# First mixer of a two-block forward pass: head projections turned from features on partitions to tokens on partitions, with the head norms along the free axis; and two steps of the opening moved

## The chip, the cores and the metric

One core of a Trainium2 chip runs the whole program in one launch. The metric is device time in microseconds (us). TensorE (PE) does the matmuls, PEld is its weight load, VectorE (DVE), ScalarE (ACT) and GpSimd (POOL) do elementwise work, and SyncE (SP) issues nearly all DMA transfers. Three runs of the kernel before took 2167.51, 2169.84 and 2172.88 us.

## The reference, cut to what matters

The program is a first transformer block, then a second block with a mixer and a mixture of experts. The change is in the first block: its mixer, and the very first norm.

```python
h = h + 0.5 * swiglu(rms_norm(h, g_ffn1[i]), ...)              # first FFN
u = rms_norm(h, g_mix[i]) @ w_in[i]                            # 512 tokens, 1024 features
q_lat, kv_lat, k_rope, qd, kd, vd = jnp.split(u, IN_OFFSETS, axis=-1)
# diff_mixer: 4 heads, two 64-wide queries and keys each, 128-wide values
q = rms_norm(qd.reshape(B, S, 4, 2, 64), g_q)
k = rms_norm(kd.reshape(B, S, 4, 2, 64), g_k)
a = softmax(q1 k1 * scale + bias) - lam * softmax(q2 k2 * scale + bias)
o = rms_norm(a @ v, g_sub) * (1 - lambda_init)
# mla_mixer: 8 heads; 64-wide nope and 32-wide rope part, each with its norm
q = (rms_norm(q_lat, g_q_lat) @ w_q_up)
kv = (rms_norm(kv_lat, g_kv_lat) @ w_kv_up)
q_nope, k_nope = rms_norm(q[..., :64], g), rms_norm(k_nope, g)
q_rot = apply_rope(rms_norm(q[..., 64:], g), cos, sin)
h = h + concat([o_mla, o_diff]) @ w_out[i]
h = h + 0.5 * swiglu(rms_norm(h, g_ffn2[i]), ...)              # second FFN
```

## The kernel before, in words

Activations are kept transposed: features on the 128 partitions, all 512 tokens along the free axis, as eight tiles h0 to h7. A matmul operand is split into a high and a low part (xs0h and xs0l, whl for weights), and one product is three matmuls, high by high, high by low and low by high (mm3, lines 400 to 402; a few low-level lines are shared by all callers, so tiles tell them apart). A weight block is a DMA of 512 KB into wraw, a copy on ACT to the high part (L377) and a subtraction for the low part, in turn on DVE (L380) and on POOL (L384).

**Opening** (setup and block1). h0 is loaded from ACT's queue, h1 to h7 from SP's. For each of the eight tiles norm_prep writes the high part on ACT (L395), the low part on DVE (L396), the square on POOL (L431) and adds it to acc on DVE (L435). The first two weight blocks (gate in psg, up in pss, 24 matmuls each) wait for these parts; eight thin matmuls with ones (L444) follow.

**First mixer** (block1, from 386 to 723 us). A projection (proj) is 24 matmuls of 512 columns, weights stationary, into one PSUM bank psg of a pool G of three; evacuate (L632) multiplies by the token's rstd, broadcast over partitions. The norm of a head is a sum over partitions, so row_rstd (L485 square on ACT, L488 thin matmuls against two indicator columns, into [token, head] form) and rsqrt give 1/rms with tokens on partitions; pairs (L462) spreads these over 128 columns, bc2 (L470) transposes them back, and diff_n (L771) and mla_n (L863, L871) multiply. Values are transposed on PE (L566), since the attention product wants tokens on partitions. The MLA heads do the same from the two latents, with a rope table on DVE (L727).

**Order.** TASKS1 lists the projections; ITEMS1 lists the eight attention items d0 to d3, m0 to m3. merge interleaves the two generators by weights in their yields, need holds an item back until its inputs are some clock units old, high_priority lifts single instructions, and the scheduler fixes one static order for each engine. The scores of an item run beside the output product of the item before; projection matmuls stand between them. In a diff item DVE does, for each of four query tiles, two bias-and-min passes (L790) and the difference (L803), ACT two exponentials (L794); the output product is L814. The pool G is used by projections, by the output products and by w_out alike.

The few lines around which the steps turn:

```python
ps = self.G()                                   # proj: one bank for a projection
self.mm3(ps, w[:, 0, c], w[:, 1, c], x[:, 0, :], x[:, 1, :], k == 0, k == kc - 1)
nc.vector.tensor_tensor(L_["y"], ps, r, op=OP.mult)          # evacuate, L632
nc.scalar.activation(sq, y, AF.Square)                       # row_rstd, L485
nc.tensor.matmul(ps[:, o : o + 2], sq[...], self.cb1[...])   # row_rstd, L488
```

Of the kernel before, what the change touches and what calls it, by code (L numbers as in the profile page):

```python
# [16 lines left out]
P = 128  # L17
T = 512
# [13 lines left out]
TASKS1 = "q1 k1 v1 v0 kv q2 k2 v2 ql0 ql1 rq q3 bq k3 ple0 rkv kr v3 wkv bkv m0 m1 ple1 m2 wo2 m3 wo3 wo0"  # L32
# [47 lines left out]
def layout(inp):  # L80
# [20 lines left out]
    cols = []  # L101
    for h in range(HD):
        cols += [oqd + h * P + ar(P), okd + h * P + ar(P), ovd + h * P + ar(P)]
    cols += [oq + ar(256), okv + ar(128), kr, krp, kr, krp]
    L["w_inA"] = _a(w_in, np.concatenate(cols))
# [9 lines left out]
    wq = _a(g["w_q_up"][0], np.concatenate(qcols))  # L115
    L["w_qup"] = np.ascontiguousarray(wq.reshape(2, 4, P, 256).transpose(0, 2, 1, 3).reshape(2, P, 1024))
# [32 lines left out]
    L["c_rt1"] = np.concatenate([c, ss, c, ss], axis=0)  # L149
# [87 lines left out]
class Prog:  # L237
# [64 lines left out]
    def setup(self):  # L302
        nc, I, base = self.nc, self.I, self.base
        self.g1 = base.tile([P, 82], F32, name="g1")
        self.h = [base.tile([P, T], F32, name=f"h{m}") for m in range(KC)]
        nc.scalar.dma_start(self.h[0], I["xT"][0])
        nc.scalar.preload_act_table_set("silu_and_others")
# [261 lines left out]
    def block1(self):  # L569
# [18 lines left out]
        rtab = self.U("rtab")  # L588
        nc.sync.dma_start(rtab, I["c_rt1"])
# [26 lines left out]
        def proj(w, evac=None, src=None, kc=KC, o=0):  # L616
            ps = self.G()
            for k in range(kc):
                c = slice(o + k * P, o + k * P + P)
                x = (xs if src is None else src)[k]  # L620
                self.mm3(ps, w[:, 0, c], w[:, 1, c], x[:, 0, :], x[:, 1, :], k == 0, k == kc - 1)
                if k % 2:
                    yield 1.3
            if evac is None and "rb" not in L_:
                L_["first"] = ps
                return
            evacuate(ps, L_["rb"] if evac is None else evac)
# [13 lines left out]

        def t_first(w):
            yield from proj(w)
            L_["r"] = self.rstd(acc2, D, "mix")

        def t_second(w):
            ps, first = self.G(), L_.pop("first")
            self.gemm(ps, w, xs, KC)
            L_["rb"] = self.bcast(L_.pop("r"), "mix")
            evacuate(first, L_["rb"])  # L650
            Y_[0] = [L_["y"]]
            evacuate(ps, L_["rb"])
            Y_[0].append(L_["y"])
            stats(("qk", 0), [(y, 0) for y in Y_[0]])
            yield

        def t_q(w, h):
            yield from proj(w)
            Y_[h] = [L_["y"]]

        def t_k(w, h):
            yield from proj(w)
            Y_[h].append(L_["y"])
            stats(("qk", h), [(y, 0) for y in Y_[h]])
            yield 1.0

        def t_v(w, h):
            yield from proj(w)
            vd[h] = self.U("vd")
            self.transposes(vd[h], L_["y"])  # L670
            mark(("v", h), 1.0)
            yield 0.4
# [32 lines left out]
        def t_b(w, k):  # L705
            L_["rb" + k] = self.bcast(L_["r" + k], k)
            yield 0.4

        def t_mla(w, p):
            if p % 2 == 0:  # L710
                L_["wq"] = w
            ql = [L_["ql", 0], L_["ql", 1]]
            ys = []
            for e in range(2):
                yield from proj(L_["wq"], L_["rbq"], ql, 2, ((2 * p + e) % 4) * 256)
                ys.append(L_["y"])
            for o in (0, 512):
                yield from proj(L_["wkv"], L_["rbkv"], [L_["kvl"]], 1, o + p * P)
                ys.append(L_["y"])
            yield 1.3  # L720
            vd["m", p] = self.U("vm")
            self.transposes(vd["m", p], ys[3])
            Y_["m", p] = ys
            stats(("m", p), [(ys[0], 1), (ys[1], 2), (ys[2], 0)])
            for e in range(2):
                rr = slice(64 * (1 - e), 64 * (1 - e) + 64)
                nc.vector.tensor_tensor(ys[e][rr], ys[e][rr], rtab[rr], op=OP.mult)  # L727
            yield 2.0
# [35 lines left out]

        def diff_n(h):
            yield from need(("qk", h))
            r = L_["qk", h]
            es = [self.pairs(r, 4, o) for o in (0, 2)]
            for y, e, g, d, n in ((Y_[h][0], es[0], gd[:, h : h + 1], q_, "dq"), (Y_[h][1], es[1], self.g1[:, GDK : GDK + 1], k_, "dk")):
                t = self.U("dn")  # L770
# [4 lines left out]
            del Y_[h]  # L775
# [31 lines left out]
        def diff_o(h):  # L807
# [3 lines left out]
            for j in range(4):  # L811
                at = self.U("at")
                self.cols(at, a, j)
                mm(po, vd[h][:, j * P : (j + 1) * P], at, start=j == 0, stop=j == 3)  # L814
                yield 1.3
# [24 lines left out]
        def mla_kr(_):  # L840
# [4 lines left out]
            nc.vector.tensor_tensor(t, t, rtab, op=OP.mult)  # L845
# [12 lines left out]
        def mla_n(p):  # L858
            yield from need(("m", p))
            ys, r = Y_.pop(("m", p)), L_["m", p]  # L860
            es = [self.pairs(r, 6, o) for o in (4, 0, 2)]
            kn = self.U("kn")
            nc.vector.scalar_tensor_tensor(kn, ys[2], self.g1[:, GMKN : GMKN + 1], self.bc2(es[0]), op0=OP.mult, op1=OP.mult)  # L863
            yield 0.4
            q_["m", p], k_["m", p] = [], []
            for e in range(2):
# [4 lines left out]
                nc.vector.scalar_tensor_tensor(t, ys[e], gs[:, e : e + 1], self.bc2(es[1 + e]), op0=OP.mult, op1=OP.mult)  # L871
# [27 lines left out]
        def mla_o(p):  # L899
            aa, r1 = M_.pop(("m", p))  # L900
            po = self.G()
            vm = vd["m", p]
            for j0 in (0, 2):
# [7 lines left out]
                for n, m in enumerate((3, 1, 2, 0)):  # L911
                    e, j, at = ats[m]
                    ins = mm(po[64 * e : 64 * e + 64], vm[:, j * P + 64 * e : j * P + 64 * e + 64], at, start=n < 2 and j0 == 0, stop=n > 1 and j0 == 2)
# [12 lines left out]
        for k in range(2):  # L926
            nc.sync.dma_start(praw[k], I["pT"][k])
        wA = I["w_inA"]
        lead = [(wA[0], t_first), (wA[1], t_second)]
        T_ = {"ql0": [(wA[12], lambda w: t_ql(w, 0))], "ql1": [(wA[13], lambda w: t_ql(w, 1))], "kv": [(wA[14], lambda w: t_kv(w, 0))],  # L930
              "kr": [(wA[15], lambda w: t_kr(w, 0))], "wkv": [(I["w_kvup"][0], lambda w: t_wkv(w, 0))]}
        for k in ("q", "kv"):
            T_["r" + k] = [(None, lambda w, k=k: t_r(w, k))]
            T_["b" + k] = [(None, lambda w, k=k: t_b(w, k))]
        for h in range(4):
            for s, f in enumerate((t_q, t_k, t_v)):
                T_["qkv"[s] + str(h)] = [(wA[3 * h + s], lambda w, f=f, h=h: f(w, h))]
            T_[f"m{h}"] = [(I["w_qup"][h // 2] if h % 2 == 0 else None, lambda w, h=h: t_mla(w, h))]
            T_[f"wo{h}"] = [(I["w_out"][h, m4], lambda w, h=h, m4=m4: t_wo(w, h, m4)) for m4 in range(2)]
        for b in range(2):  # L940
# [1241 lines left out]
```

## Time and profile before

| | us |
|---|---|
| median of three runs | 2169.84 |
| the profiled execution, its own time | 2170.61 |
| its span, first to last instruction | 2168.8 |
| PE busy in the span | 2104.8 (97%) |
| DVE, ACT, POOL busy | 957.9, 715.1, 557.1 |
| mean granted TensorE clock | 0.988 of full speed |

The profile is of one execution; busy shares say little where stages differ, so the stretches are read one by one. Durations of single matmuls overlap, since PE pipelines them; the distance between starts is what one costs. A matmul with f32 operands is recorded twice.

### The profile page before, as it was taken

How to read it: one execution, taken by the hardware profiler on the slowest of the kernel's cores; microseconds unless marked ns; L12 is line 12 of the kernel's file. 1: busy time of each engine (PE TensorE's matmuls, PEld its weight loads, DVE VectorE, ACT ScalarE, POOL GpSimd, SP SyncE). 2: the span in 40 equal slices, each digit the busy share in tenths (PEclk: the TensorE clock that was granted, in tenths of full speed). 3: DMA queues.
4: the chain of work that ended last, by engine and by line, in shares of the span. 5: the costliest groups of instructions: out<-in, count | busy, mean ns of one | idle time of the engine just before them, and what ended most of it. 6: DMA issues, size and time to landing. Idle time of an engine off the chain costs nothing.

```text
span 2168.8 us, 25911 instructions
## 1 busy us (share of the span) xinstructions
PE 2104.8 (97%) x10233; PEld 1511.1 (70%) x10233; DVE 957.9 (44%) x1695; ACT 715.1 (33%) x1193; POOL 557.1 (26%) x457
## 2 busy tenths in 40 slices
PE   7999999999899999999998999999999999999997
PEld 5888888777676788888777877667887455545544
DVE  5323334465675532323476995553253232323322
ACT  3223223445644422222344667442231111111112
POOL 4323224423421532323443445111230000000000
PEclk9999999999999999999999999999999999999999
DMA  4223333311010232333322111112626899999994
GB/s 153 93 93 97 97 97 107 120 64 51 19 49 20 89 96 88 97 97 98 110 86 75 50 37 47 30 49 69 235 67 248 351 400 414 421 411 410 413 391 163
DMA packets 67838, 330.73 MB, mean 152 GB/s; under 512 B 7792, under 2 KB 8960, under 8 KB 43648
## 3 DMA queue, kind: packets, MB, share of 16 engines
q1 hardware_dynamic: 66992, 327.71, 40.9%
q8 instruction: 82, 1.34, 0.3%
q10 hardware_dynamic: 720, 1.31, 0.2%
q14 instruction: 44, 0.36, 0.1%
HBM read 326.90 MB, written 2.10 MB: 152 GB/s over the span
## 4 chain that ended last, share of the span: by engine, by line


## 5 line engine op out<-in xcount | busy, mean ns | idle before, releaser
L384 POOL TENSOR_TENSOR whl<-wraw,whl 128x512 fp32r<-128x512 f32 x228 | 306.4, 1364 | 598.0 <-ACT whl L377 366.7
L377 ACT ACTIVATE whl<-wraw 128x1024 fp32r<-128x1024 f32 (+1 forms) x227 | 237.1, 1045 | 638.5 <-PE psg L402 264.6
L380 DVE TENSOR_TENSOR whl<-wraw,whl 128x1024 fp32r<-128x1024 f32 (+1 forms) x113 | 157.0, 1389 | 60.1 <-ACT whl L377 59.9
L2045 POOL TENSOR_TENSOR fr<-fv,mhalf 128x1 f32<-128x1 f32 x4 | 2.2, 544 | 513.9 <-DVE fv L2044 512.2
L1745 PE MATMUL pss<-mw,xe 128*64 128x512 f32 x512 | 115.3, 592 | 0.0
L1745 PE MATMUL pss<-mw,hT 128*64 128x512 f32 x480 | 109.7, 611 | 0.5 <-ACT hT L1923 0.5
L526 POOL TENSOR_TENSOR t<-t,t 128x512 f32<-128x512 f32 x44 | 57.2, 1300 | 202.0 <-DVE t L525 194.4
L1745 PE MATMUL psg<-mw,xe 128*64 128x512 f32 x480 | 108.1, 592 | 0.0
L525 DVE TENSOR_TENSOR t<-pss,rb_f 128x512 f32<-128x512 f32 x44 | 30.4, 690 | 162.8 <-PE pss L402 162.8
L558 DVE SCALAR_TENSOR_TENSOR h<-pst,h 128x512 f32<-128x512 f32 x48 | 33.2, 691 | 140.3 <-PE pst L402 140.3
L2018 DVE TENSOR_TENSOR h<-h,psg 128x512 f32<-128x512 f32 x120 | 81.1, 685 | 23.0 <-PE psg L1745 23.0
L1905 DVE SCALAR_TENSOR_TENSOR mt<-pss,sc,mt 128x512 f32<-128x512 f32 x16 | 12.0, 750 | 179.1 <-PE pss L1745 178.6
L1745 PEld LDWEIGHTS pss<-mw,xe 128*64 128x64 f32 x512 | 36.7, 137 | 73.1 <-issue 73.1
L1745 PEld LDWEIGHTS psg<-mw,xe 128*64 128x64 f32 x480 | 34.4, 137 | 68.2 <-issue 64.6
L1745 PEld LDWEIGHTS pss<-mw,hT 128*64 128x64 f32 x480 | 33.9, 140 | 65.1 <-issue 60.9
L396 DVE SCALAR_TENSOR_TENSOR yel<-pss,sc,yeh 128x512 fp32r<-128x512 f32 x32 | 24.0, 751 | 121.5 <-ACT yeh L395 121.5
L1745 PE MATMUL pst<-disp,uhh 128*128 128x256 f32 x256 | 66.7, 287 | 1.2 <-DVE disp L1823 1.2
L523 DVE TENSOR_TENSOR t<-psg,rb_f 128x512 f32<-128x512 f32 x44 | 30.4, 690 | 81.6 <-PE psg L402 76.0
L1745 PE MATMUL pst<-disp,uhl 128*128 128x256 f32 x256 | 65.2, 281 | 0.0
L1904 ACT ACTIVATE mt<-psg,sc 128x512 f32<-128x512 f32 x16 | 11.0, 687 | 157.1 <-PE psg L1745 134.2
L435 POOL TENSOR_TENSOR acc<-acc,sq 128x512 f32<-128x512 f32 x33 | 49.9, 1512 | 39.6 <-ACT sq L433 35.8
L395 ACT ACTIVATE yeh<-pss,sc 128x512 fp32r<-128x512 f32 x32 | 22.0, 688 | 115.1 <-PE pss L1745 105.0
(889 smaller groups left out, 5625.5 us busy)
## 6 DMA issues: line engine op xcount, KB each, us to landing
mw<-in_w SPq DMA_DIRECT2D x188, 1024.0 KB, 9.2
wraw<-in_w_gu SPq DMA_DIRECT2D x87, 512.0 KB, 3.5
wraw<-in_w_d SPq DMA_DIRECT2D x48, 512.0 KB, 3.5
wraw<-in_w2A SPq DMA_DIRECT2D x38, 512.0 KB, 3.5
wraw<-in_w_inA SPq DMA_DIRECT2D x16, 512.0 KB, 3.5
wraw<-in_w_out SPq DMA_DIRECT2D x8, 512.0 KB, 3.5
wraw<-in_w_pg SPq DMA_DIRECT2D x8, 512.0 KB, 3.6
wraw<-in_w_up SPq DMA_DIRECT2D x8, 512.0 KB, 3.4
```

The source lines that it names most:

```text
L377: nc.scalar.activation(hl[:, 0, :n], raw[:, :n], AF.Copy)
L380: nc.vector.tensor_sub(hl[:, 1, :n], raw[:, :n], hl[:, 0, :n].bitcast(F32))
L384: nc.gpsimd.tensor_sub(hl[:, 1, c], raw[:, c], hl[:, 0, c].bitcast(F32))
L395: nc.scalar.activation(hi, src, AF.Identity, scale=scale)
L396: nc.vector.scalar_tensor_tensor(low, src, scale, hi.bitcast(F32), op0=OP.mult, op1=OP.subtract)
L435: (eng or nc.gpsimd).tensor_add(acc, acc, t)
L523: nc.vector.tensor_tensor(t1, pg, rb, op=OP.mult)
L525: nc.vector.tensor_tensor(t2, pu, rb, op=OP.mult)
L526: nc.gpsimd.tensor_tensor(t2, t1, t2, op=OP.mult)
L558: nc.vector.scalar_tensor_tensor(self.h[m], py, 0.5, self.h[m], op0=OP.mult, op1=OP.add)
L1745: return self.next_to(nc.tensor.matmul(*args, **kw))
L2018: self.nc.vector.tensor_tensor(self.h[m], self.h[m], ps, op=OP.add)
```

## The change

All of the edits are in the first block.

- **Projections of the diff heads.** Query and key of one head form a block of 256 columns, and the values of two heads another: six blocks (w_inB), each of two weight loads, the first for input tiles 0 to 3 and the second for 4 to 7. t_block makes the activations stationary (128 tokens) and streams 256 weight columns: 96 matmuls of 256 columns into two banks of G, for four token tiles. The latents, the shared rope key and their loads (w_inA) stay as they were.
- **Norms.** squares takes the square on ACT straight from the bank and sums groups of 64 on DVE (TENSOR_REDUCE); qk multiplies by the square of the token's rstd, takes rsqrt, and scaled writes both banks times 1/rms. turned then transposes the normalised tiles, and split applies the gain on the way out of PSUM.
- **Values.** values evacuates with a per-partition scale on ACT; no transposition follows.
- **MLA.** t_up does the same from the latents, for queries of four heads (mq0, mq1), all keys (mk) and all values (mv), one bank for each token tile; the rope table is applied with the gain in mla_n.
- **Opening.** h0 comes from SP's queue, after the first half of the first weight block, and the squares are on ACT.
- **Order.** TASKS1 has a new list; the broadcasts of the latents' rstd (bq, bkv) are gone.

```diff
-TASKS1 = "q1 k1 v1 v0 kv q2 k2 v2 ql0 ql1 rq q3 bq k3 ple0 rkv kr v3 wkv bkv m0 m1 ple1 m2 wo2 m3 wo3 wo0"
+TASKS1 = "qk1 v0 kv qk2 v1 ql0 ql1 rq qk3 ple0 rkv kr wkv mk mq0 mv ple1 mq1 wo2 wo3 wo0"
...
-        nc.scalar.dma_start(self.h[0], I["xT"][0])
...
-            for m in ((1,), (2, 3))[a]:
+            for m in ((0,), (1, 2, 3))[a]:
...
-        t = acc if first else self.U("sq")
-        if eng is nc.vector:
-            nc.gpsimd.tensor_tensor(t, src, src, op=OP.mult)
+        if first:
+            nc.scalar.activation(acc, src, AF.Square)
         else:
+            t = self.U("sq")
             nc.scalar.activation(t, src, AF.Square)
-        if not first:
             (eng or nc.gpsimd).tensor_add(acc, acc, t)
...
+        def t_block(w, s, then=None):
+            if s == 0:
+                L_["tm"] = [self.G() for _ in range(2)]
+            for i in range(4):
+                ps = L_["tm"][i // 2][:, (i % 2) * 256 : (i % 2) * 256 + 256]
+                tk = slice(i * P, i * P + P)
+                for k in range(4):
+                    c = slice(k * 256, k * 256 + 256)
+                    x = xs[4 * s + k]
+                    first, last = s + k + i % 2 == 0, s + i % 2 == 2 and k == 3
+                    mm(ps, x[:, 0, tk], w[:, 0, c], start=first, stop=False)
+                    mm(ps, x[:, 1, tk], w[:, 0, c], start=False, stop=False)
+                    mm(ps, x[:, 0, tk], w[:, 1, c], start=False, stop=last)
+                yield 1.4
+            if s:
+                then(L_.pop("tm"))
+        def squares(src, ms):
+            sq = self.U("sq")
+            with self.tc.high_priority(offset=HP1):
+                nc.scalar.activation(sq, src, AF.Square)
+                nc.vector.tensor_reduce(ms, sq.rearrange("p (s f) -> p s f", f=64), axis=AX.X, op=OP.add)
+        def scaled(out, src, r):
+            with self.tc.high_priority(offset=HP1):
+                nc.vector.tensor_tensor(out.rearrange("p (s f) -> p s f", f=64), src.rearrange("p (s f) -> p s f", f=64),
+                                        r.unsqueeze(2).to_broadcast([P, 8, 64]), op=OP.mult)
+        def qk(h):
+            def then(pss):
+                v, r = self.S("ms", 16), self.S("rr", 16)
+                for b, ps in enumerate(pss):
+                    squares(ps, v[:, 8 * b : 8 * b + 8])
+                ...
+                    self.rsqrt(r, v)
+                ...
+                Y_[h] = [self.U("y") for _ in range(2)]
+                for b, ps in enumerate(pss):
+                    scaled(Y_[h][b], ps, r[:, 8 * b : 8 * b + 8])
+                mark(("qk", h), LAG)
+            return then
...
+                        nc.scalar.activation(t[:, c], ps[:, c], AF.Copy, scale=rx[0][:, 2 * b + i : 2 * b + i + 1])
...
+        def t_up(w, lat, o, key, then):
+            for i in range(4):
+                ps = self.G()
+                tk = slice(i * P, i * P + P)
+                for k, x in enumerate(lat):
+                    c = slice(o + k * 512, o + k * 512 + 512)
+                    self.mm3(ps, x[:, 0, tk], x[:, 1, tk], w[:, 0, c], w[:, 1, c], k == 0, k == len(lat) - 1)
+                y = self.U("vm" if then is None else "ym")
...
+                    nc.scalar.activation(y, ps, AF.Copy, scale=L_[key][:, i : i + 1])
+                ...
+                    squares(y, v[:, 8 * i : 8 * i + 8])
...
+        def turned(ys, o, w):
+            ps = self.PT()
+            n = 512 // w
+            for i in range(4):
+                c = (i % n) * w + o
+                nc.tensor.transpose(ps[:, i * P : i * P + P], ys[i // n][:, c : c + P], self.ident)
+            return ps
...
-            es = [self.pairs(r, 4, o) for o in (0, 2)]
...
-                nc.vector.scalar_tensor_tensor(t, y, g, self.bc2(e), op0=OP.mult, op1=OP.mult)
-                self.split(d[h], t, lo=nc.gpsimd)
+                self.split(d[h], turned(ys, o, 256), scale=g)
```

On PE, among the first projections of the mixer: before, the key projection of head 1 has the thin matmuls of another tile's square (L488) between its own.

Before:

```order
L400 MATMUL psg<-xs5h,whl 128x512
L488 MATMUL pst<-cb_2512,sq 128x2 x4
L401 MATMUL psg<-xs5l,whl 128x512
L402 MATMUL psg<-xs5h,whl 128x512
L400 MATMUL psg<-xs6h,whl 128x512
```

After, from the block of head 0 into the block of head 1, with the broadcast of the token's rstd (r_mix) between:

```order
L649 MATMUL psg<-whl,xs7h 128x256
L650 MATMUL psg<-whl,xs7l 128x256
L651 MATMUL psg<-whl,xs7h 128x256
L454 MATMUL pst<-ident,r_mix 128x128 x4
L649 MATMUL psg<-whl,xs0h 128x256
L650 MATMUL psg<-whl,xs0l 128x256
```

And after, the transpositions of head 1 and the first scores behind them (dkh and dqh are the split key and query):

```order
L651 MATMUL psg<-whl,xs7h 128x256
L825 MATMUL pst<-ident,y 128x128 x8
L414 MATMUL pss<-dkh,dqh 128x512 x2
```

The thin matmuls are gone, and a block goes straight on into the next.

On DVE, the chain of head 1 (ms are the sums of squares, nw and rr the steps of rsqrt, whl a weight split, dql and dkl the low parts of head 0). Before:

```order
L632 TENSOR_TENSOR y<-psg,rb_mix 128x512
L491 TENSOR_SCALAR rv<-pst 128x16
L365 TENSOR_TENSOR nw<-rr 128x16
L366 SCALAR_TENSOR_TENSOR nw<-nw,rv 128x16
L367 SCALAR_TENSOR_TENSOR rr<-nw,rr 128x16
L632 TENSOR_TENSOR y<-psg,rb_mix 128x512
L462 COPY bce<-rr 128x512 x2
```

After:

```order
L661 TENSOR_REDUCE ms<-sq 128x8
L676 TENSOR_TENSOR ms<-ms,rx_2620 128x16
L677 TENSOR_SCALAR ms<-ms 128x16
L379 TENSOR_TENSOR whl<-wraw,whl 128x1024
L364 TENSOR_TENSOR nw<-rr 128x16
L365 SCALAR_TENSOR_TENSOR nw<-nw,ms 128x16
L366 SCALAR_TENSOR_TENSOR rr<-nw,rr 128x16
L679 TENSOR_TENSOR rr<-rr,r_mix 128x16
L666 TENSOR_TENSOR y<-psg,rr 128x512 x2
```

The bank is read for the last time at the end of the chain now; before, it was read once, by the first row, ahead of it.

On POOL and ACT in the opening. POOL before, after its first three squares:

```order
L384 TENSOR_TENSOR whl<-wraw,whl 128x512 x2
L431 TENSOR_TENSOR sq<-h_85 128x512
L431 TENSOR_TENSOR sq<-h_86 128x512
L431 TENSOR_TENSOR sq<-h_87 128x512
L431 TENSOR_TENSOR sq<-h_88 128x512
```

ACT after:

```order
L394 ACTIVATE xs3h<-h_86,g_82 128x512
L376 ACTIVATE whl<-wraw 128x1024
L432 ACTIVATE sq<-h_86 128x512
L394 ACTIVATE xs4h<-h_87,g_82 128x512
L432 ACTIVATE sq<-h_87 128x512
```

Each square now stands on ACT between two high parts.

## Rows read from the trace of the kernel before

**Rows 1.** The page, part 1: busy time and share of the span.

```profile
PE 2104.8 (97%) x10233; PEld 1511.1 (70%) x10233; DVE 957.9 (44%) x1695; ACT 715.1 (33%) x1193; POOL 557.1 (26%) x457
```

**Rows 2.** Busy time by stretch over the first mixer: start:end, length, engines, PEclk.

```profile
543.00:557.00 14.00, 12.81 (x72) 11.79 (x70) 8.83 (x18) 7.25 (x16) 6.55 (x5) 0.64 0.05 20
557.00:592.00 35.00, 30.04 (x138) 19.30 (x138) 25.13 (x69) 22.56 (x52) 15.97 (x14) 1.00 0.05 16
...
sum 337.00, PE 322.08 PEld 238.32 DVE 209.26 ACT 168.25 POOL 105.96; mean PE 46.01 PEld 34.05 DVE 29.89 ACT 24.04 POOL 15.14
570.00:580.00 10.00, 7.60 (x40) 5.27 (x41) 8.33 (x25) 6.61 (x14) 1.97 (x3) 1.00 0.01 2
```

**Rows 3.** Timeline of the opening: start, duration, engine, line, operation.

```profile
12.98 1.75 DVE L396 SCALAR_TENSOR_TENSOR xs3l<-h,g,xs3h 128x512 fp32r<-128x512 f32 x1
14.14 6.82 POOL L431 TENSOR_TENSOR sq<-h 128x512 f32<-128x512 f32 x5
...
23.30 0.74 DVE L396 SCALAR_TENSOR_TENSOR xs7l<-h,g,xs7h 128x512 fp32r<-128x512 f32 x1
...
28.44 0.95 PE L444 MATMUL pst<-ones,acc 128*128 128x1 f32 x8
```

**Rows 4.** Groups by line and shape, PE, 386 to 723 us: count, busy, mean, idle.

```profile
L488 PE MATMUL pst<-cb,sq 128*128 128x2 f32 x168 | 23.0, 263 | 0.4 <-DVE rv L491 0.4
L566 PE MATMUL pst<-ident,y 128*128 128x128 f32 x32 | 5.1, 281 | 0.3 <-DVE y L632 0.2
...
L456 PE MATMUL pst<-ident,r_q 128*128 128x128 f32 x4 | 0.7, 285 | 1.7 <-POOL r_q L449 1.7
L456 PE MATMUL pst<-ident,r_kv 128*128 128x128 f32 x4 | 0.6, 272 | 0.0
```

**Rows 5.** PE timeline: the same kinds at both levels of the clock.

```profile
409.97 1.03 PE L470 MATMUL pst<-ident,bce 128*128 128x128 f32 x8
...
553.25 3.08 PE L470 MATMUL pst<-ident,bce 128*128 128x128 f32 x12 [0.82 <-DVE bce L462]
...
637.75 0.63 PE L402 MATMUL psg<-oT6h,whl 128*128 128x512 f32 x1
...
642.02 0.63 PE L400 MATMUL psg<-oT6h,whl 128*128 128x512 f32 x1
```

**Rows 6.** PE rows of 264 and 512 columns; weight loads of 128.

```profile
1139.78 0.28 PE L400 MATMUL psg<-xs1h,whl 128*128 128x264 f32 x1
...
1141.48 0.28 PE L402 MATMUL psg<-xs5h,whl 128*128 128x264 f32 x1
...
385.84 0.39 PE L400 MATMUL psg<-xs0h,whl 128*128 128x512 f32 x1
...
390.22 0.39 PE L401 MATMUL psg<-xs6l,whl 128*128 128x512 f32 x1
...
L400 PEld LDWEIGHTS pss<-kth,mqh 128*128 128x128 f32 x32 | 6.0, 188 | 4.1 <-ACT am L891 1.9 <-DVE mn L790 1.7
```

**Rows 7.** Groups and DVE rows that price the new chain and the scoring.

```profile
L485 ACT ACTIVATE sq<-y 128x512 f32<-128x512 f32 x21 | 12.8, 624 | 4.1 <-DVE y L632 4.0
L377 ACT ACTIVATE whl<-wraw 128x1024 fp32r<-128x1024 f32 x30 | 31.7, 1056 | 45.7 <-PE psg L402 37.0 <-issue 6.4 <-POOL whl L384 2.1
...
L889 DVE TENSOR_REDUCE mn<-pss 128x1 f32<-128x512 f32 x32 | 21.4, 684 | 14.4 <-PE pss L402 13.5 <-ACT am L891 0.9
L632 DVE TENSOR_TENSOR y<-psg,rb_mix 128x512 f32<-128x512 f32 x16 | 10.8, 686 | 14.2 <-PE psg L402 14.1
...
404.25 0.17 DVE L491 TENSOR_SCALAR rv<-pst 128x16 f32<-128x16 f32 x1 [2.57 <-PE pst L488]
...
405.37 0.17 DVE L367 SCALAR_TENSOR_TENSOR rr<-nw,rr 128x16 f32<-128x16 f32 x1
...
424.87 0.69 DVE L790 CUSTOM_DVE_ANT_0 sb<-pss,dist 128x512 f32<-128x512 f32 x1
...
428.42 0.68 DVE L790 CUSTOM_DVE_ANT_0 sb<-pss,dist 128x512 f32<-128x512 f32 x1
```

More of the change, by code (lines that the diff above doesn't have):

```diff
@@ L100, in layout @@
     krp = okr + np.concatenate([ar(16, 32), ar(16)])
[L101 to L105, printed above, removed]
+    L["w_inA"] = _a(w_in, np.concatenate([oq + ar(256), okv + ar(128), kr, krp, kr, krp]))
+    blocks = [np.concatenate([o + h * P + ar(P) for o in (oqd, okd)]) for h in range(HD)] + [ovd + v * 256 + ar(256) for v in range(2)]
+    L["w_inB"] = np.concatenate([w_in[:, c].reshape(2, 4, P, 256).transpose(0, 2, 1, 3).reshape(2, P, 1024) for c in blocks])
     qcols = []
@@ L148, in layout @@
     L["c_b1"] = np.concatenate([sl.reshape(P, 10), rk], axis=1)
-    L["c_rt1"] = np.concatenate([c, ss, c, ss], axis=0)
+    one = np.ones((64, T), np.float32)
+    L["c_rt1"] = np.stack([np.concatenate([one, c, ss], axis=0), np.concatenate([c, ss, one], axis=0)])
     dist = np.abs(p[:, None] - ar(896)[None, :] + 384).astype(np.float32)
@@ L587, in block1 @@
         nc.sync.dma_start(self.cb1, I["c_b1"])
-        rtab = self.U("rtab")
-        nc.sync.dma_start(rtab, I["c_rt1"])
+        rtab = [self.U("rtab") for e in range(2)]
+        for e in range(2):
+            nc.sync.dma_start(rtab[e], I["c_rt1"][e])
         gs = self.base.tile([P, 4], F32, name="gs")
@@ new lines, in values, with then @@
+        def values(v):
+            def then(pss):
+                for b, ps in enumerate(pss):
+                    t = self.U("vd")
+                    for i in (0, 1):
+                        c = slice(256 * i, 256 * i + 256)
+                        nc.scalar.activation(t[:, c], ps[:, c], AF.Copy, scale=rx[0][:, 2 * b + i : 2 * b + i + 1])
+                    for h in (2 * v, 2 * v + 1):
+                        for i in (0, 1):
+                            vd[h, 2 * b + i] = t[:, 256 * i + P * (h % 2) : 256 * i + P * (h % 2) + P]
+                for h in (2 * v, 2 * v + 1):
+                    mark(("v", h), 1.0)
+            return then
@@ L674, in t_ql @@
+        rx = []
+        def t_first(w):
+            yield from t_block(w, 0)
+            r = self.rstd(acc2, D, "mix")
+            r2 = self.S("rx2")
+            nc.vector.tensor_tensor(r2, r, r, op=OP.mult)
+            nc.vector.tensor_scalar(r2, r2, 1.0 / 64, None, op0=OP.mult)
+            rx.extend((r, r2))
+        def t_second(w):
+            yield from t_block(w, 1, qk(0))
+            L_["rb"] = self.bcast(rx[0], "mix")
         def t_ql(w, c):
@@ L703, in t_r @@
             yield 0.5
[L705 to L712, printed above, removed]
-            ys = []
[L714 to L728, printed above, removed]
+        def t_up(w, lat, o, key, then):
+            ys = []
+            for i in range(4):
[5 more added lines that the diff above has]
+                y = self.U("vm" if then is None else "ym")
+                with self.tc.high_priority(offset=HP1):
+                    nc.scalar.activation(y, ps, AF.Copy, scale=L_[key][:, i : i + 1])
+                ys.append(y)
+                yield 0.7 * len(lat)
+                if then is not None:
+                    if i == 0:
+                        v = self.S("ms", 32)
+                    squares(y, v[:, 8 * i : 8 * i + 8])
+            if then is None:
+                vd["m"] = ys
+                return
+            r = self.S("rr", 32)
+            with self.tc.high_priority(offset=HP1):
+                nc.vector.tensor_scalar(v, v, 1.0 / 64, EPS, op0=OP.mult, op1=OP.add)
+                self.rsqrt(r, v)
+            for i, y in enumerate(ys):
+                scaled(y, y, r[:, 8 * i : 8 * i + 8])
+            Y_[then] = ys
+            mark(then, LAG)
@@ L730, in t_wkv, with t_mq, t_mk, t_mv @@
+        def t_mq(w, b):
+            yield from t_up(w, [L_["ql", 0], L_["ql", 1]], 0, "rq", ("mq", b))
+        def t_mk(w, _):
+            yield from t_up(L_["wkv"], [L_["kvl"]], 0, "rkv", "mk")
+        def t_mv(w, _):
+            yield from t_up(L_["wkv"], [L_["kvl"]], 512, "rkv", None)
         def t_wkv(w, _):
```

82 lines of the change are left out of this document (30 added, 52 removed).

## The prediction

> **What bounds the kernel now.** I read the page's busy shares first. PE is busy for 2104.8 of 2168.8 us [rows 1], so time is won by taking work off PE, by filling a stretch in which it waits, or by a faster clock. The second view is busy time by stretch, over the changed mixer, 386 to 723 us. PE is busy for 322.08 of 337.00 us [rows 2], so it waits for 14.9 us. Two stretches stand out. From 543 to 557 us PE is nearly always busy, yet the granted clock is 0.64 of full speed; from 557 to 592 us it waits for 35.00 - 30.04 = 5.0 us at full clock. Third, the timeline of the opening [rows 3]: the low part xs3l takes 1.75 us on DVE while POOL has work, xs7l takes 0.74 once POOL has none, and the thin matmuls that close the opening start at 28.44 us. Last, the groups of PE by line and shape [rows 4], for what the change removes and adds.
>
> **Terms of the mixer: what goes.**
> The thin matmuls for the head norms (L488) take 23.0 us of PE for 21 tiles, each 4 matmuls recorded twice, 168 rows [rows 4]. One tile, the rope key, stays: 23.0 x 20/21 = 21.9 us. The transpositions of values take 5.1 us. The two broadcasts of the latents' rstd take 0.7 + 0.6 us, and the first is preceded by a wait of 1.7 us for POOL: 3.0 us.
> The 80 transpositions of spread 1/rms and the 80 of normalised tiles cancel: same count, same 128x128 f32 shape.
> The clock: behind a long run of thin matmuls it is at the lower of its two levels, 1.2 instead of 2.4 GHz. Twelve transpositions took 3.08 us there, 0.257 each, against 1.03 for eight, 0.129 each, elsewhere: 12 x 0.128 = 1.5 us. After the last such run, w_out matmuls start ten steps apart in 642.02 - 637.75 = 4.27 us, 0.427 each, where 0.231 is usual: 10 x 0.196 = 2.0 us [rows 5]. With the runs gone, this goes as well: 3.5 us.
> Sum: 21.9 + 5.1 + 3.0 + 3.5 = 33.5 us.
>
> **What comes on PE.** 288 matmuls of 512 columns become 576 of 256. The trace has 264 columns with a weight load for each: 14 steps in 1141.48 - 1139.78 = 1.70 us, 0.121 each, or 0.118 for 256 if scaled by columns. For 512 columns it is 19 steps in 390.22 - 385.84 = 4.38 us, 0.231 each [rows 6]. So 576 x 0.118 - 288 x 0.231 = 68.0 - 66.5 = 1.5 us. The lower end is the same columns at the same price, 0. The upper end takes the recorded weight load, 188 ns, as not hidden: 576 x 0.188 - 66.5 = 42 us. The 264-column rows are nearly the changed shape, so I take 1.5. MLA and latent projections keep their matmuls.
>
> **What comes as waits.** This is the term that I had to estimate. A diff block holds two of the three banks of G, and the banks are now read at the end of the norm's chain instead of at its start. The next block has one free bank, good for two token tiles of four input tiles: 24 matmuls, 2.8 us. The chain after a block's last matmul, from rows [rows 7]: square 0.62, sum on DVE 0.68 (priced by the reduction of scores), two small steps 0.2, from rv to the end of rr 405.54 - 404.25 = 1.3, one small step 0.2, first scaled write 0.69: 3.7 us. A weight copy stands in ACT's row ahead of the logarithm, 1.06 us, and after heads 0 and 1 its subtraction in DVE's row behind it: 5 us in all. Behind PE's wait everything else of PE stands, scores included.
> - Head 0 into head 1 and head 1 into values: 5.0 - 2.8, less some transpositions, 2.0 us each.
> - Head 2 into values: 3.7 + 0.1 - 2.8 = 1.0 us, since no weight subtraction stands in that chain on DVE and the copy is early.
> - Head 3 into the embedding projection (pT): there the free bank is good for 6 matmuls only, 1.4 us, and four thin ones, 0.4. The chain also has an evacuation in it: 3.7 + 1.06 + 0.6 - 1.8 = 3.5 us.
> Together 8.5 us; nothing at the least, and about twice that if DVE and ACT are late.
> Scoring: DVE needs 428.42 - 424.87 = 3.55 us for one query tile [rows 7], 14.2 for an item. The first diff item used to have more than 7 us of projections beside it. Now PE has 24 matmuls of scores (5.5 us at 0.231, and less since two halves run side by side; 4.5), 24 narrow matmuls (2.8) and 24 wide (5.5), 12.8 us, and must wait for the third query tile's DVE work before it may go on: 2.5 us with the lag of the first tile. Of the 168 narrow matmuls that follow, nearly all stand ahead of the second item's output product and few beside it: 2.5. The third item has fewer wide matmuls beside it: 2. The fourth, with the first MLA item, has next to none, as before: 5.
> The keys, queries and values from the latents: 12 tiles, each with an evacuation on ACT at about the price of a square, and eight squares of 0.62, some 12 us beside 48 matmuls, 11 us: 2. The rest, where two product chains at the end lose the w_out matmuls that stood behind them: 6.5 us, against 5.2 before.
> Sum: 8.5 + 2.5 + 2.5 + 2 + 5 + 2 + 6.5 = 29 us, against 14.9 - 1.7 = 13.2 that the old stretch has without the wait counted above. Net 15.8 us lost.
>
> **Off the path.** DVE loses 28 evacuations of 0.69 and the spreading copies and gains 20 sums and 20 scaled writes at about the same price; ACT gains some 10 us and POOL loses eight low parts. PE covers these: in the whole mixer DVE works 209 and ACT 168 of 337 us [rows 2]. Where the cover is thin, in scoring, I have priced it. On SP's queue there is one more table of 256 KB and the loads are in another order; the same number of weight blocks follows at the same pace, behind PE.
>
> **The opening.** From xs3l to xs7l DVE takes 23.30 - 12.98 = 10.3 us for four steps of one low part and one sum [rows 3]. At 0.74 + 0.68 less overlap, 1.3 us each, as after POOL is done, it is 5.2: 5.1 us less. POOL still splits the second weight block then, which may cost 1 us. h0 comes as the third of SP's loads instead of from ACT's queue, so the first matmul may be later by some 0.3 us; ACT does 0.62 and about 0.7 per tile, 1.3,, which does not become the bound. I take 4 us; the ends are -1 (ACT's row in order, each high part behind a square) and 6. The stretch behind it is full of PE work, so what is won stays won.
>
> **Sum.** 33.5 - 1.5 - 15.8 + 4 = 20.2 us. The profiled execution took 2170.6 us (the median of three is 2169.8, within 0.04%), so I forecast 2150.
>
> **A rule that speaks against it.** In [rows 2] PE waits for a quarter of 570 to 580 us and the granted clock is 1.00; it is low where PE was busy with thin matmuls. The Trainium skill, page "TensorE: Matmul & The Clock Gate", section "A second HAM failure mode: psum-queue depth-cycling", says that a kernel that cycled through PSUM banks paused often enough between groups of matmuls to send the clock back and forth. By that the new bank waits would cost more than their length, rival two; the rows so far bear it out little.
>
> **The rivals.**
> 1. *The waits do not come*, since DVE and ACT run the chains early: 33.5 - 1.5 + 4 = 36 us, 2134. For it: DVE is busy for less than two thirds. Against it: the order shows blocks one behind another with three banks. 0.10.
> 2. *Slower: the bank waits lower the clock.* Place: the six diff blocks. A narrow matmul at the lower level costs 0.118 more (the wide ones went from 0.231 to 0.427). The gain of 20.2 us is gone from 171 of the 576 on; with half of them, 34 us more, it is 2184. For it: 0.64 in 543 to 557 us shows that this mixer can lose the clock. Against it: waits of 1 to 2 us at a clock of 1.00. 0.07.
> 3. *Slower: weight loads are not hidden* behind 256 columns: 42 instead of 1.5 us, 2190. Against it are the 264-column rows. 0.03.
> 4. *The waits eat the gain*: waits of 13.2 + 33.5 - 1.5 + 4 = 49 us in all instead of 29 would leave nothing; I put the case at 46 us, 2167. For it: four in-order engines in one chain. 0.13.
> 5. *The opening gives nothing*, mixer as forecast: 2154, within the forecast's own range.
>
> **How the numbers follow.** Forecast with its neighbours, 0.67: its own range is 2142 to 2160. What a measurement of this kernel can tell from no change is about 0.3%, 6.5 us. Faster: 0.67 and 0.10 = 0.77. Same: 0.12 of rival four. Slower: 0.07, 0.03 and the rest of rival four, 0.11. The range of 8 in 10 takes in most of rivals one and four: 2137 to 2168.
>
> **What would show it.** L488 left with 8 rows; 576 rows of 256 columns with starts 0.118 apart; PE waits behind DVE's scaled writes (L666), four of them of 1 to 4 us; the closing thin matmuls of the opening near 24 us; no stretch of 10 us in the mixer below 0.8 of the clock. It is wrong if block matmuls start 0.2 us apart, if PE's waits in the mixer pass 49 us, or if the mixer's stretch is no shorter than 330 us.

## The result and the profile after

The changed kernel takes 2195.1 us (2193.9 to 2195.6, four runs) against 2170.4 of before on the same chip: ratio 1.0114, 95% interval 1.0099 to 1.0129. It is 25 us slower where 2150, 20 us faster, was forecast.

The page's busy shares of after answer to [rows 1]:

```profile
PE 2104.8 (96%) x10321; PEld 1516.3 (69%) x10321; DVE 956.8 (44%) x1681; ACT 727.9 (33%) x1217; POOL 536.5 (24%) x441
```

PE's busy time is the same to the digit although work was taken off it. Busy time over the first mixer, from its first projection to the FFN behind it, says why; the line is start:end, length, PE, PEld, DVE, ACT, POOL, granted clock, DMA. First before:

```profile
385.84:715.10 329.26, 314.34 (x1564) 232.02 (x1562) 203.65 (x449) 163.90 (x327) 99.55 (x78) 0.97 0.17 54
```

Then after, whole and in three parts:

```profile
379.62:738.65 359.03, 313.23 (x1652) 237.46 (x1650) 204.87 (x435) 172.92 (x343) 86.71 (x69) 0.91 0.16 50
...
379.62:430.00 50.38, 49.81 (x370) 44.54 (x369) 28.56 (x73) 21.39 (x37) 11.84 (x10) 1.00 0.38 128
430.00:600.00 170.00, 136.43 (x673) 104.24 (x669) 87.60 (x208) 78.69 (x155) 43.41 (x34) 0.84 0.14 44
600.00:738.65 138.65, 126.99 (x614) 88.68 (x613) 88.71 (x156) 72.84 (x154) 31.46 (x25) 0.98 0.10 29
```

The mixer starts 6.2 us earlier, which is the opening's gain, and takes 29.8 us longer. PE waits 45.8 us in it (359.03 - 313.23), 30.9 more than before; and it is busy as long as before, with less work, since the clock is lower. Most of both stands between 430 and 600 us: 33.6 us of waits and a clock of 0.84.

The waits of PE in after, 370 to 760 us (what waits, for whom, us in all, times, the longest):

```profile
PE pst L825 <- DVE ym L666: 7.2, 2, 4.5
PE pss L414 <- DVE mn L849: 6.7, 6, 1.6
PE psg L399 <- ACT pp L797: 5.1, 2, 4.3
PE pst L442 <- POOL accq L433: 3.6, 1, 3.6
...
PE psg L649 <- DVE y L666: 2.3, 3, 1.9
...
PE psg L399 <- DVE y L666: 1.6, 1, 1.6
PE psg L649 <- ACT vd L692: 1.6, 1, 1.6
```

The last three are the waits for the banks of the blocks, on which the prediction spent 8.5 us: 5.5. The large ones are elsewhere: the MLA queries (ym), the scores (mn, their row minima on DVE), the embedding projection (pp), and the sum of squares of the query latent (accq).

The clock is lost behind them. Ten-microsecond stretches of after:

```profile
470.00:480.00 10.00, 7.49 (x19) 3.93 (x19) 3.85 (x15) 5.02 (x12) 0.00 (x0) 0.66 0.02 7
480.00:490.00 10.00, 10.00 (x33) 8.10 (x33) 1.96 (x7) 2.20 (x6) 0.20 (x1) 0.66 0.01 2
490.00:500.00 10.00, 6.53 (x39) 5.59 (x38) 5.50 (x6) 3.89 (x7) 4.55 (x3) 1.00 0.24 64
500.00:510.00 10.00, 9.88 (x58) 9.88 (x58) 1.39 (x2) 1.06 (x1) 1.08 (x2) 0.66 0.11 43
...
580.00:590.00 10.00, 4.02 (x16) 3.01 (x16) 9.07 (x12) 4.86 (x8) 6.18 (x5) 0.50 0.00 1
```

From 500 to 510 us PE is busy all the time and gets 58 matmuls done; it had waited 3.6 us just ahead, at a clock still shown as 1.00.

TensorE's clock has two levels in these traces, a granted share of 1.00 and of 0.50 (2.4 and 1.2 GHz). Seven stretches of the mixer of after are at the lower one, two of before; their sums, after and then before:

```profile
sum 61.40, PE 51.09 PEld 38.74 DVE 29.45 ACT 28.88 POOL 19.59; mean PE 7.30 PEld 5.53 DVE 4.21 ACT 4.12 POOL 2.80
sum 17.00, PE 15.98 PEld 13.84 DVE 8.16 ACT 5.26 POOL 3.98; mean PE 7.99 PEld 6.92 DVE 4.08 ACT 2.63 POOL 1.99
```

At half the clock about half of PE's time there is lost: some 25.5 us in after against 8.0 before. All seven stretches begin during a wait of PE of 1.0 us or more, or within 2.5 us of its end; the two of before begin behind thin matmuls (L488), with no such wait ahead. Not every wait is followed by one: after waits of 1.9 us at 449 us and of 1.6 at 519 the clock stays at 1.00.

### The profile page after: what moved, and what is told of

The parts are those of the page before. It is cut to its first block, busy times and chain, and to the rows that moved or that the text cites. A ratio compares the mean times of both kernels' runs of the same rounds, so it can differ in the third digit from the quotient of the medians.

```text
span 2193.8 us, 26067 instructions
## 1 busy us (share of the span) xinstructions
PE 2104.8 (96%) x10321; PEld 1516.3 (69%) x10321; DVE 956.8 (44%) x1681; ACT 727.9 (33%) x1217; POOL 536.5 (24%) x441
## 4 chain that ended last, share of the span: by engine, by line
PE 80%; DVE 8%; issue 4%; ACT 4%; POOL 2%; DMA 0%; SPq 0%; DVEq 0%; ACTq 0%; POOLq 0%
PE pss L1809 10%; PE psg L399 8%; PE psg L400 8%; PE psg L401 8%; PE psg L1809 8%; PE pss L399 4%; PE pss L401 4%; PE pss L400 4%; PE pst L400 4%; PE pst L399 4%; PE pst L401 4%; PE pst L1809 4%; ACT whl L376 1%; PE psg L649 1%; PE psg L650 1%
```

## The experiments

All times are medians beside runs of the kernel before on the same chip. The chips differ a little: before took 2170.4 us beside after, 2169.6 beside e1 to e4, 2166.9 beside e5 to e8, 2168.9 beside e9 to e12 and 2168.1 beside e13. So runs of different groups are compared by their ratios to before, good to some 4 or 5 us, and by the mixers of their profiled executions.

**Which half loses.** Two kernels split the change. The first is the kernel before with only the edits of `setup` and `sumsq` (e1); the second is the changed kernel with before's `t_mla`, `mla_n`, `mla_o` and broadcasts, and their tasks in its list (e2).

> The kernel before with only the opening of the change (loads of the activations on SP, squares on ACT); its first mixer is that of before. In the changed kernel's trace the closing thin matmuls of the opening start at 21.65 us instead of 28.44, and the mixer starts 6.2 us earlier. All theories agree here: 6 to 7 us faster than before, about 2164, the mixer's stretch 329 us as before. If it is less than 4 us faster, the opening's gain is partly taken back later, and the mixer's loss is smaller than 30 us.

2161.3 us, ratio 0.9969 (0.9955 to 0.9983): 6.7 us won, its mixer takes 327.6 us with 14.9 us of waits. The whole loss against this kernel, 31 us by the ratios, is the mixer's (359.0 against 327.6 us).

> The changed kernel with only the differential heads (and the opening) in the new layout; the MLA heads with their projections, broadcasts and norms as before. It says in which half the mixer's 30 us are lost. Matmul work goes down by 8 of 20 norm tiles (8.8 us) and 4 of 8 value transpositions (2.6 us). If the loss lies in the MLA half (the queues of ACT and DVE around 570 to 616 us): mixer about 329 - 11 + 7 = 325 us, in all 2158 to 2163. If it lies in the differential half, where PE waits for 20.5 us before 560 us in the changed kernel: mixer about 345 us, in all 2178 to 2185. If it is shared, as the waits by stretch say (20.5 us to 560, 25.3 behind): about 335 us, 2170.

2191.6 us, mixer 357.2: the differential half in its place in the order brings the loss by itself, above the range that I gave for that case. The MLA half adds 3 us to it, which is within the noise.

**The order or the chains.** One rule of `merge` altered: an attention that waits for its input falls back in turn, and does not catch up afterwards with scores alone.

```
                 d = next(g[i])
+                if d is None and spread:
+                    t[i] = max(t[i], t[1 - i] * w[i] / w[1 - i])
```

> The changed kernel with one rule of the merge altered in the first mixer: an attention that had to wait for its input is not allowed to catch up with scores back to back afterwards, so projections stand between the scores. Same instructions, other order. Theory A (the order: scores stand in bursts without projections beside them, PE waits there, and the low clock follows the waits): PE's waits in the mixer fall from 45.8 to 25 us and half of the time at the low clock comes back, 10 us, less some 5 us in which the last MLA scores have no w_out beside them: 2165 to 2175. Theory B (the chains of the new layout on ACT and DVE are longer wherever they stand): 2188 to 2200. Theory C (the low clock comes from the narrow matmuls and not from the waits): waits fall but the clock stays, 2178 to 2184.

2158.7 us, ratio 0.9951 (0.9935 to 0.9968): some 35 us less than after with the same instructions, more than theory A had asked. Mixer of this kernel, and two stretches of its second item's scores:

```profile
380.16:703.75 323.59, 300.71 (x1651) 228.47 (x1650) 202.43 (x435) 171.69 (x343) 86.42 (x69) 0.96 0.17 56
...
460.00:470.00 10.00, 9.50 (x43) 6.31 (x40) 5.20 (x20) 5.60 (x14) 2.52 (x2) 1.00 0.17 54
470.00:480.00 10.00, 10.00 (x48) 7.18 (x46) 7.16 (x16) 6.38 (x12) 0.00 (x0) 1.00 0.15 54
```

Waits fall to 22.9 us, and PE's busy time by 12.5 us although no matmul went: from 470 to 480 us it does 48 instead of 19, at 1.00 instead of 0.66. The chains of the new layout are not what costs; theory B is out. So is theory C: with the same narrow matmuls the clock over the mixer is 0.96 instead of 0.91.

**Is the low clock the price of the waits?** Useless matmuls where PE waits in after, result overwritten: two ahead of each transposition group of the differential product chains (e4), seven ahead of the thin matmuls of the query latent (e11).

```
         ps = self.PT()
+        for i in range(2 if fill is not None else 0):
+            self.nc.tensor.matmul(ps, self.ident, fill, start=True, stop=True)
```

> The changed kernel with two idle matmuls (f32, 512 columns, some 0.46 us each, result overwritten) ahead of each transposition group of the differential product chains: 32 of them, 14.7 us of useless PE work at places where PE now waits for the scores' DVE work. Theory A (the low clock follows the waits): the waits shrink by nearly as much, the stretches 470 to 487, 547 to 558 and 590 to 612 us are at the high clock, and the kernel is no slower, 2185 to 2195. Theory B (waits alone cost): waits shrink, clock as before, 2195 to 2200. Theory C (low clock from something else, waits set by another engine's row): 2200 to 2210.

2196.6 us. I had taken one such matmul for 0.46 us; four records, that is two matmuls, take 1.82 from the first start to the next instruction's, so it was 29 us of useless work. The ratio is 1.0124 (1.0107 to 1.0141) against 1.0114 of after, no difference clear of noise; the profiled mixer is 364.2 us, 5.1 longer. Stretch 452 to 490 us, after and then filled:

```profile
452.00:490.00 38.00, 33.04 (x156) 24.18 (x155) 16.72 (x53) 14.94 (x33) 2.70 (x3) 0.82 0.11 36
```

```profile
452.00:490.00 38.00, 37.65 (x176) 25.84 (x175) 21.17 (x56) 16.50 (x35) 2.75 (x3) 0.96 0.15 43
```

The scores' waits for mn are gone, 13.0 us of wait in all, and the clock there is 0.96. Thirteen of 29 us went into waits and 5 into time; the other 11 came back as clock. The time lies where theory B had it, but B wanted the clock as before, and over the mixer it rose from 0.91 to 0.94.

> The changed kernel with seven idle matmuls (f32, 512 columns, 0.91 us each by the fill run, 6.4 us in all) ahead of the thin matmuls for the query latent, in a bank that is overwritten later. 22 narrow matmuls (2.6 us) stand behind that place instead of ahead of it, so the fill covers 2.6 + 3.6 us, all of the wait. If the low clock follows the wait: the 96 narrow matmuls start 0.118 apart, 0.1 + 6.4 + 0.9 + 11.3 = 18.7 us where the changed kernel takes 19.4, and 6.4 us of useless work cost nothing, 2192 to 2196. If the clock falls there for another reason: 74 of them are 0.04 to 0.12 slower as before, 3 us more, 2197 to 2201.

2194.8 us, ratio 1.0123 (1.0107 to 1.0140) against 1.0114: the time cannot tell the two outcomes apart, which lie 3 us from each other. The trace can. The timeline of the fill, then busy time in the stretch behind it:

```profile
493.35 6.17 PE L650 MATMUL psg<-rtab,ident 128*128 128x512 f32 x14
499.59 1.05 PE L442 MATMUL pst<-ones,accq 128*128 128x1 f32 x8
...
500.82 0.28 PE L654 MATMUL psg<-whl,xs1h 128*128 128x256 f32 x1
500.93 0.29 PE L655 MATMUL psg<-whl,xs1l 128*128 128x256 f32 x1
```

```profile
500.00:510.00 10.00, 10.00 (x86) 10.00 (x86) 1.56 (x3) 1.66 (x2) 1.02 (x1) 1.00 0.13 38
```

86 matmuls in the ten microseconds that had 58, the narrow ones 0.12 apart. At this place the low clock followed the wait: with the wait filled, the same narrow matmuls run at 1.00, and 6.2 us of work for nothing cost nothing that the runs can tell.

**Single places.** The task rq moved behind qk3 (e6); low parts of the MLA keys on DVE, the two `lo=nc.gpsimd` of `kt` struck out (e7); in `t_up` the square issued ahead of the `yield` (e9).

```
-TASKS1 = "... ql0 ql1 rq qk3 ple0 ..."
+TASKS1 = "... ql0 ql1 qk3 rq ple0 ..."
```

> The changed kernel with one task moved: the query latent's rstd (rq) behind the fourth head's block instead of ahead of it. In the changed kernel PE waits 3.6 us there for POOL's sum of squares, and the clock is low for some 10 us behind it (74 narrow matmuls in 11.4 instead of 8.8 us). If a wait costs its own length and the clock behind it: 6 us less, 2189. If only its length: 2191.5. If the wait covered others that now come late instead: 2194 to 2196. Some order behind it changes as well, so 2 us either way tells nothing.

2183.6 us, some 8.5 less by the ratios (1.0075 against 1.0114); the wait for accq is gone, and 490 to 510 us are at a clock of 1.00. Its mixer is 8.9 us shorter, 4.5 of it waits and 4.4 PE's busy time:

```profile
380.23:730.39 350.16, 308.83 (x1651) 233.66 (x1650) 203.34 (x435) 172.91 (x343) 86.90 (x69) 0.92 0.16 52
```

So the place cost over twice its wait of 3.6 us, more than I expected; as the order behind it changes too, the share of this one wait is not shown.

> The changed kernel with the low parts of the MLA keys (rope and nope halves) made on DVE instead of POOL. PE's order up to there is the same. In the changed kernel POOL has five of them in a row, 1.26 us each, from 572 to 579 us, a copy on ACT waits 2.41 us for the last, and DVE's four scaled writes take 4.64 instead of 2.5 us beside POOL's sums; PE waits 4.3 and 7.2 us. If the waits at 570 to 587 us are those of POOL's row: they shrink by 4 to 6 us and with the clock behind them it is 6 to 9 us faster, 2186 to 2189. If ACT's row (six high parts of 0.63 ahead of the square) is what counts: 0 to 2 us, 2193 to 2195.

2196.0 us, no gain. The wait for ym falls from 7.2 to 4.3 us, but 2.1 us return in front of the next scores (mqn, am). POOL's row was not what counted.

```
-                yield 0.7 * len(lat)
                 if then is not None:
                     ...
                     squares(y, v[:, 8 * i : 8 * i + 8])
+                yield 0.7 * len(lat)
```

> The changed kernel with one statement moved: in the MLA projections a tile's square is issued ahead of the point where the merge may insert attention, not behind it. In the changed kernel the last query tile is copied at 563.2 us but squared at 574.2, behind six high parts of the MLA keys in ACT's row, and PE waits 4.5 and 2.7 us for the scaled writes at the end of that chain. If ACT's row in order is what makes PE wait there: these 7.2 us go, and with the clock behind them it is 8 to 12 us faster, 2183 to 2187. If the copies of the embedding projection (4.3 us) or the scores behind take the wait over: 2191 to 2195.

2183.8 us, some 10 less by the ratios (1.0067 against 1.0114). Its mixer is 8.3 us shorter, nearly all of it waits (37.7 instead of 45.8 us); PE's busy time is the same, so the clock, which the expectation had in its sum, gave nothing back:

```profile
379.73:730.44 350.71, 313.00 (x1652) 237.03 (x1650) 207.68 (x435) 172.16 (x343) 85.90 (x69) 0.92 0.17 52
```

ACT in after, start and duration: the tile is copied at 563.16 us and squared eleven microseconds later, behind the high parts of the MLA keys.

```profile
563.16 0.67 ACT L756 ACTIVATE ym<-psg,r_q 128x512 f32<-128x512 f32 x1
...
570.43 0.63 ACT L391 ACTIVATE kth<-krs 64x512 fp32r<-64x512 f32 x1
571.08 0.63 ACT L391 ACTIVATE kth<-kn 64x512 fp32r<-64x512 f32 x1
571.74 1.28 ACT L391 ACTIVATE kth<-krs 64x512 fp32r<-64x512 f32 x2
...
574.23 0.61 ACT L660 ACTIVATE sq<-ym 128x512 f32<-128x512 f32 x1
574.75 0.56 ACT L797 COPY pp<-psg 128x512 f32<-128x512 f32 x1
...
576.57 0.23 ACT L361 ACTIVATE rr<-ms 128x32 f32<-128x32 f32 x1 [0.59 <-DVE ms L768]
579.21 0.58 ACT L797 COPY pp<-psg 128x512 f32<-128x512 f32 x1 [2.41 <-POOL ktl L392]
579.69 0.23 ACT L362 ACTIVATE rr<-rr 128x32 f32<-128x32 f32 x1
```

The same tile with the square ahead of the merge point:

```profile
562.96 0.67 ACT L756 ACTIVATE ym<-psg,r_q 128x512 f32<-128x512 f32 x1
563.53 0.68 ACT L756 ACTIVATE vm<-psg,r_kv 128x512 f32<-128x512 f32 x1
564.10 0.63 ACT L660 ACTIVATE sq<-ym 128x512 f32<-128x512 f32 x1
...
567.29 0.24 ACT L361 ACTIVATE rr<-ms 128x32 f32<-128x32 f32 x1
567.56 0.23 ACT L362 ACTIVATE rr<-rr 128x32 f32<-128x32 f32 x1
```

In after even the exponential at 579.69 stands behind a copy that waits for another engine. The Trainium skill, page "PSUM — Partial Sum Buffer", section "Engine vs sequencer instructions", says that ACT's, DVE's and POOL's queues are strictly in order; these rows agree.

**Are these parts of one sum?** Both edits that helped, e6's and e9's, under the old merge rule.

> The changed kernel with the two single edits that each gave 11 us (rq behind the fourth head's block; the MLA projections' square ahead of the merge point) and nothing else; the merge rule is the old one, so the scores still stand in bursts. If the two places are separate parts of the loss: 2195.1 - 11.5 - 11.3 = 2172, which leaves 11 us against the opening alone (2161.3) for the bursts of scores, and the spread order's further 13 to 19 us are their price. If both edits took the same wait out: 2180 to 2184. If mending two places brings the old merge level with the spread one: 2158 to 2163, and the bursts cost nothing.

2178.2 us, ratio 1.0041 (1.0026 to 1.0056): some 16 us won of the 19 that the two give singly by their ratios, 15.4 of 17.2 by the mixers. They are separate parts, as far as the noise lets one tell. Some 16 us remain against the opening alone. PE still waits 31.5 us in this mixer, 6.0 of it for mn, and its busy time is hardly less than after's 313.2, at a clock of 0.92: what the two edits mend is waits, not the clock.

```profile
379.89:723.52 343.63, 312.13 (x1652) 235.25 (x1650) 206.35 (x435) 172.42 (x343) 86.15 (x69) 0.92 0.17 53
```

**The layout in a mended order.** The old layout under the altered rule (e5); the spread run with rq late and e7's edit (e8), then e9's as well (e10); the differential half alone, spread and rq late (e12).

> The kernel before with the opening of the change and the altered merge rule of the spread run, but with head projections in the old layout. It is the control for the spread run (2158.7 us, mixer 323.6): does the new layout win once its order is mended, or was all of it the rule? If the rule helps only the new layout (whose blocks are longer and leave the scores bare): no better than opening alone, 2161, mixer 328 us or more. If the rule would have helped any layout: 2140 to 2150, and the new layout is then worth nothing or less in itself. With equal shares: 2153.

2170.5 us, ratio 1.0014 (1.0004 to 1.0025) against 0.9969: the rule makes the old layout some 10 us slower than the opening alone, 4.2 of it in the mixer (331.8 against 327.6). It is not a better rule; it suits the new layout.

> The spread run with both single edits: rq behind the fourth head's block, low parts of the MLA keys on DVE. In the spread run PE still waits 22.9 us in the mixer, 1.4 of it for POOL's sum of squares, and 2.9 for the MLA queries' scaled writes. If single waits add up: 2153 to 2156. If the mended order already hides them: 2157 to 2160, no difference.

2152.9 us, ratio 0.9940 (0.9924 to 0.9957), faster than both kernels; from the spread run's 0.9951 it is not told apart. Its mixer:

```profile
379.81:699.76 319.95, 294.80 (x1651) 223.45 (x1650) 210.00 (x447) 171.00 (x343) 70.08 (x57) 0.98 0.18 57
```

Here PE's busy time falls by 19.5 us against before. Waits are 25.2 us, above the spread run's 22.9; the clock went from 0.96 to 0.98. Against the opening alone (0.9969, mixer 327.6) the new layout is worth some 6 us by the ratios, 7.7 by the mixers; the prediction had 16 for it.

> The best so far (spread merge, rq later, low parts of the MLA keys on DVE; 2152.9 us) with the square of the MLA projections issued ahead of the merge point as well. There, PE's waits for the MLA queries are 2 to 5 us. If the row of ACT still delays the chain in the spread order: 2147 to 2151. If the spread order hides it: 2151 to 2155.

2158.2 us (2150.7 to 2159.4), ratio 0.9948 (0.9935 to 0.9961): not to be told from e8.

> The run with only the differential heads in the new layout (2191.6 us), now with the spread merge rule and rq later. It says whether the MLA half is worth its change once the order is mended: the spread run with the same two edits and the low parts on DVE took 2152.9. If the MLA half gains what it removes, 12 of 20 norm tiles and 4 transpositions (13.2 + 2.6 us) less some waits: 2160 to 2168 here. If it gains nothing: 2150 to 2156. If this order is bad for the old MLA tasks, as it was for the old layout as a whole (9 us worse): 2170 or more.

2172.3 us, ratio 1.0018 (1.0008 to 1.0027), mixer 339.2: 17 us slower than e8 by the ratios, 19 by the mixers. That is the third case of the expectation, in which this order is bad for the old MLA tasks. So these 17 to 19 us, with e7's edit in them, are not shown to be the worth of the MLA half.

## Why the prediction was wrong

**What goes: right in kind, priced some 4 us too high.** Eight rows of 128x2 are left (L486), the value transpositions and the broadcasts are gone. But [rows 4] gives busy time, which counts the overlap of a group's ends with its neighbours. From start to start, less PE's waits, the 168 rows of L488 take 21.0 us in the trace of before and not 23.0, the value transpositions 3.4 and not 5.1, the broadcasts 0.8 and not 1.3.

**What comes on PE: right.** The 576 narrow matmuls start 0.118 to 0.120 apart where the clock is high. Rival three, weight loads not hidden, did not happen.

**The opening: right, a little low.** 6.2 us at the mixer's start, 6.7 by the run alone; forecast 4. The closing thin matmuls of [rows 3] come at 21.65 us, and the low parts on DVE that stand beside POOL's work no more take 0.74 (xs4l, beside POOL's split of a weight block, still 1.78):

```profile
15.42 0.74 DVE L395 SCALAR_TENSOR_TENSOR xs5l<-h,g,xs5h 128x512 fp32r<-128x512 f32 x1
...
21.65 0.95 PE L442 MATMUL pst<-ones,acc 128*128 128x1 f32 x8
```

**What comes as waits: the step that failed.** 29 us forecast, 45.8 measured. Not at the blocks' banks (8.5 forecast, 5.5 measured), but where I had given little or nothing: keys, queries and values from the latents and what stands beside them, 2 us forecast, 11.5 for ym and pp at 570 to 587 us; and rq, booked as a wait of 1.7 us that goes, is one of 3.6. I read the order for PE's banks only and not the rows of ACT and POOL; there the late square and the late sum of squares could be seen.

**The clock: failed with it.** I booked 3.5 us won. PE's busy time should have fallen by 30.3 us (33.5 less the old wait of 1.7 and less the 1.5 added); it fell by 1.1. Those 29 us are the larger half of the error of 45. Some 17.5 of them are the added work at the lower level (25.5 less 8.0), 3.5 the gain that did not come, 4 the prices of what goes; the last 4 no run divides. I had priced every wait at its own length, since [rows 2] show a stretch with waits at a clock of 1.00. These were single waits of 0.2 to 1.2 us, not the 1 to 2 that rival two names; the longest of the old mixer, 1.7 us at 490, also left the clock at 1.00. The fills show that waits here cost the clock as well, at the places filled, and the spread run that with the waits halved 12.5 us of busy time come back. The two late chains cost mainly their waits: e6 gave back 4.4 us of busy time, e9 none. Even in e8, with no more work at the lower level than before (13.5 us against 16.0), busy time fell by 19.5 and not by 30.3.

**The rivals.** Rival two gave the right sign and the mechanism, and with 2184 a time 11 us short. Its place was mostly wrong: of the seven stretches at the lower level only the one at 432 us begins in a wait for the bank of a diff block; the others stand behind waits in scores without projections beside them, in the late chains and in later items. The rule that I weighed there and found little borne out, in the Trainium skill, page "TensorE: Matmul & The Clock Gate", section "A second HAM failure mode: psum-queue depth-cycling", agrees in kind: PE pauses between groups of score matmuls, for 1.1 to 1.6 us each from 464 to 473 us, and the clock falls to its lower level at 473 us. That the pauses come from cycling through banks no run here shows. Rival four had the waits right at 46 us and no loss of clock. The conditions for "wrong" that the prediction named came true in the stretch (359 against 330 us, where before has 329 between the same ends), not in the waits (45.8 against 49). The sign that no ten microseconds fall below 0.8 of the clock failed too, at 0.66 and 0.50.

**What stays open.** Why a wait of 2 us costs the clock at one place and not at another is not settled: the wait of 1.9 us for a block's bank at 449 us leaves it at 1.00 in after, and in the spread run the same wait, at 445 us, is followed by the lower level from 447.5 on. How the 16 us that e13 leaves divide between bursts of scores and the rest is argued from the spread run, which changes the whole order. Why the best order wins 8 us in the mixer where 16 were forecast was not tested beyond the prices above.

## What to carry to other kernels

Work taken off the bounding engine was here also what covered the others' chains: after such a change the order has to be set anew, and both together be measured; the same instructions were 25 us slower than before in one order and 11 faster in another, 7 of these 11 from the opening. Reckon a wait on TensorE at its length, and as a second case with slower matmuls behind it, and look in the in-order rows of all engines for a late link that now nothing covers. Price what is taken away by the distance between starts, not by busy time. To see whether a wait costs the clock, fill it with useless matmuls and read the granted clock behind it; the time alone does not say, since PE stood still there anyway.

## What was not expected of the hardware

Useless matmuls for 29 us made the mixer 5.1 us longer, and 6.2 us of them cost nothing that the runs can tell. Two f32 matmuls of 512 columns by a 128x128 f32 weight take 1.82 us, recorded as four, where the split matmuls (fp32r) of that size start 0.231 apart [rows 6]. Four scaled writes on DVE (L666) took 4.64 us beside POOL's sums and 2.50 where POOL was idle:

```profile
561.36 2.50 DVE L666 TENSOR_TENSOR ym<-ym,rr 128x512 f32<-128x512 f32 x4
...
581.94 4.64 DVE L666 TENSOR_TENSOR ym<-ym,rr 128x512 f32<-128x512 f32 x4
```
